# Weight slabs of the Fourier and convolution stage, split in the first feed forward and kept in DRAM as two parts

## The chip, the cores and the metric

The kernel runs on one core of one Trainium2 chip. The metric is device time in microseconds (us); 2587.58 us is the median of three runs of the kernel before (2584.76 to 2590.12).

## What is computed

Two blocks follow one another on a sequence of 512 positions and 1024 features. The first has two layers of attention. The second, where the change lies, has two layers: a mixer and a convolutional feed forward each. The mixer of its second layer is the Fourier and convolution stage. Cut to that layer, the reference is:

```python
h = _rmsnorm(x, norm_g[l, 0]) * (1.0 + scale) + shift
p = h @ cd_w_in                                # 1024 x 1536
y_c = _fourier_mix(p[..., :512])               # real part of a 2D FFT, 4 groups of 128
y_d = _conformer_conv(p[..., 512:], ...)       # val * sigmoid(gate), 31 taps, layer norm, silu
x = x + gate * (concat([y_c, y_d]) @ cd_w_out)
shift, scale, gate = _adaln(c, ada_w[l, 1], ada_b[l, 1])
h = _rmsnorm(x, norm_g[l, 1]) * (1.0 + scale) + shift
x = x + gate * _conv_ffn(h, ffn_w_up[l], ...)  # (silu(dwconv(u)) * v) @ w_down, 2816 wide
```

## The kernel before

All products run on TensorE in fp32r, and each factor is split into a high part (a cast on ScalarE) and a low part (a subtraction, mostly on VectorE). mm3 (L128) makes three products of these: high by high, high by low, low by high.

A weight slab is [128, 8, 128] in fp32, 512 KB. wslab (L70) loads it from SP's queue into wraw, casts it into whi (L75) and subtracts into wlo (L76). wraw, whi and wlo have three buffers each. gemm (L90) takes a slab, asks side() for one more step of waiting side work, and makes 24 matmuls of 512 columns into one of two pg buffers.

The order in which the kernel's text calls things is not the order on the engines. When the program is built, a planner sets one list for each engine and for SP's queue: among the instructions whose inputs and buffers it takes to be ready, the one earliest in the text goes first. On the chip each engine runs its list in order, and one that waits holds back what stands behind it.

The first feed forward (ffn, L1518, with l = 0) has two halves. Each makes eleven pairs of upward gemms (taps3 in L743 to L745, Silu in L1533, product in L1535, split into hidh and hidl) and then eight downward products. Beside it runs adaln (L710) as side work: 48 times a transfer of 512 KB into adaw (two buffers) and one reduction on VectorE (L719). They give the modulation that the norm at the feed forward's end needs. That norm (Norm, L239) prepares the first three slabs of the next stage in finish (L314), the third with its low part on GpSimd, between the high and low parts hh and hl of the normed input (L336, L344).

Then comes the Fourier and convolution stage (m3, L1834). conformer_in (L1411) makes eight gemms with slabs of cd_w_in; fourier (L1483) loads and splits the Fourier matrix into DH and DL in four pieces and makes four groups of one gemm, a product with CH and CL (split fuh, ful in L125) and a product with DH and DL; conformer_conv (L1428) makes the 31 taps on VectorE (cacc, L1451 and L1453), and 23 taps of the last channel on TensorE with diagonals (cdg, L1443 on GpSimd) that lie in the buffers of hh and hl; conformer_norm (L1458) follows. The projection with cd_w_out (out_proj_steps, L191) runs in two halves with half slabs (n = 4), the last three of the second half together. The loop over the two layers is at L1848.

Of the kernel before, what the change touches and what calls it, by code (L numbers as in the profile page):

```python
# [17 lines left out]
S = 512  # L18
# [6 lines left out]
class Ctx:  # L25
# [43 lines left out]

    def wslab(self, src, shape, raw=None, eng=None, out=None):  # L70
        nc = self.nc
        if raw is None:
            raw = self.wraw(src, shape)
        hi, lo = out or [self.w.tile(shape, F32R, name=t, tag=t) for t in ("whi", "wlo")]
        nc.scalar.activation(hi, raw, AF.Copy)  # L75
        (eng or nc.vector).tensor_tensor(lo, raw, hi.bitcast(F32), op=ALU.subtract)  # L76
        return hi, lo
# [113 lines left out]
    def out_proj_steps(self, pool, W, k0, mix, xcol, gate=None, done=None, norm=None, parts=None):  # L191
        nc, n = self.nc, len(mix)
        if parts is None:
            mh = pool.tile([128, n, S], F32R, name="mh")
            ml = pool.tile([128, n, S], F32R, name="ml")
            for k in range(n):
                self.split(mh[:, k, :], ml[:, k, :], mix[k])
        else:
            mh, ml = parts
        yield  # L200
        late = 0 if norm is None else norm.late if n == 8 else 3
        for o in range(KD - late):
            xc = xcol(o)
            ps = self.gemm(W[:, o, k0:k0 + n], mh, ml, n)
            self.add_x(xc, ps, gate, o)
            if done is not None:
                done(o, xc)
            if norm is not None:
                norm.tile(o)
            yield  # L210
        if norm is not None and not late:
            norm.finish()
        if late:
            last = range(KD - late, KD)
            ws = [self.wslab(W[:, o, k0:k0 + n], [128, n, 128]) for o in last]
            ps = [pp.tile([128, S], F32, name="pl", tag=tag) for pp, tag in ((self.pg, "pg"), (self.pg, "pg"), (self.px, "px"))[:late]]
            for hf, t in enumerate(HALVES):
                for j, o in enumerate(last):
                    self.products(ps[j], ws[j], (mh, ml), t, n)
                    self.add_x(xcol(o)[:, t], ps[j][:, t], gate, o)  # L220
                    norm.half(o, hf)
                if hf:
                    norm.begin()
                norm.stats(hf)
            norm.finish()
# [8 lines left out]
def at(x, k):  # L234

    return x[k] if isinstance(x, list) else x[:, k, :]


class Norm:  # L239
# [1171 lines left out]
def conformer_in(c, dp, hh, hl):  # L1411

    nc, I = c.nc, c.ins
    hds = []
    for j in range(4):
        ps = c.gemm(I["cd_w_in"][:, 8 + j], hh, hl)
        sg = c.t2("csg")
        nc.scalar.activation(sg, ps, AF.Sigmoid)
        ps = c.gemm(I["cd_w_in"][:, 4 + j], hh, hl)
        hd = dp.tile([128, S + 30], F32, name=f"chd{j}")  # L1420
        nc.gpsimd.memset(hd[:, 0:15], 0.0)
        nc.gpsimd.memset(hd[:, 527:542], 0.0)
        nc.vector.tensor_tensor(hd[:, 15:527], ps, sg, op=ALU.mult)
        hds.append(hd)
    return hds
# [57 lines left out]
def fourier(c, dp, hh, hl, mixf):  # L1483
# [1 line left out]
    DH = dp.tile([128, 8, S], F32R, name="DH")  # L1485
    DL = dp.tile([128, 8, S], F32R, name="DL")
    for z in range(4):
        raw = c.w.tile([128, 2, S], F32, name="wraw", tag="wraw")
        nc.sync.dma_start(raw, I["dft_s"][:, 2 * z:2 * z + 2])
        c.split(DH[:, 2 * z:2 * z + 2], DL[:, 2 * z:2 * z + 2], raw)  # L1490
    craw = c.load(dp, "dft_c", [128, 256])
    CH = dp.tile([128, 256], F32R, name="CH")
    CL = dp.tile([128, 256], F32R, name="CL")
    c.split(CH, CL, craw)
    for g in range(4):
        ps = c.gemm(I["cd_w_in"][:, g], hh, hl)
        uf = c.t2("fu")
        nc.scalar.activation(uf, ps, AF.Copy)
        uh = dp.tile([128, S], F32R, name="fuh", tag="fuh", bufs=2)
# [15 lines left out]

def ffn(c, fp, l, hh, hl, xT, norm):  # L1518
    nc, I = c.nc, c.ins
    gate = c.mod[l, 1][:, 2, :]  # L1520
    cw = fp.tile([128, NFF, 3], F32, name="fcw")
# [3 lines left out]
    for hf in range(2):  # L1525
        hid = []
        for jj in range(11):
            j = 11 * hf + jj
            ps = c.gemm(I["ffn_up"][l][:, 2 * j], hh, hl)
            p = padded(c, fp, ps)  # L1530
            u = c.t2("fu")
            taps3(c, u, p, cw[:, j, 0:1], cw[:, j, 1:2], cw[:, j, 2:3], cb[:, j:j + 1])
            nc.scalar.activation(u, u, AF.Silu)  # L1533
# [16 lines left out]

        for o in range(KD - late):
            c.side()
            w1 = c.wslab(W[:, o, k0:k0 + 8], [128, 8, 128])
            w2 = c.wslab(W[:, o, k0 + 8:k0 + 11], [128, 3, 128])
            ps = c.pg.tile([128, S], F32, name="pg", tag="pg")
# [36 lines left out]
def build(tc, I, out):  # L1592
    nc = tc.nc
    with ExitStack() as es:
# [238 lines left out]

        def m3(hh, hl, em, side, spec):  # L1834
            mixf = c.pool(em, "mixf", side).tile([128, KD, S], F32, name="mixf")
            W, gate = I["cd_w_out"], c.mod[1, 0][:, 2, :]
            mp = c.pool(em, "mp", side)
            with ExitStack() as e2:
                dp = c.pool(e2, "cd", side)
# [8 lines left out]
        for l, mx in enumerate((m2, m3)):  # L1848
            ex.close()
            prev = nm  # L1850
            with ExitStack() as em:
                mx(prev.hh, prev.hl, em, B, (*modulation(c, l, 1), [I["ffn_up"][l][:, k] for k in range(3)]))
            prev = nm
            if l == 0:
                nm = Norm(c, hp, xT, None, None, [I["cd_w_in"][:, k] for k in (8, 4, 9)])
            else:
                nm = Final(c, out, xT, gvec(I["final_g2"]), None, None)
            with ExitStack() as e2:
                fp = c.pool(e2, "ffn", B)
                if l == 0:  # L1860
                    sc = silu_c(fp)
                    place = lambda: fp.tile([128, 1024], F32, name="adaw", tag="adaw", bufs=2)
                    c.fill += [adaln(c, sc, 1, 0, place), adaln(c, sc, 1, 1, place)]
                for _ in ffn(c, fp, l, prev.hh, prev.hl, xT, nm):
                    if l == 0:
                        c.side(48)
                        nm.g, nm.shift = modulation(c, 1, 0)
# [178 lines left out]
```

## Time and profile before

| | |
|---|---|
| median of three runs | 2587.58 us (2584.76 to 2590.12) |
| profiled execution, its own time | 2596.75 us |
| its span | 2594.9 us |
| TensorE matmul busy | 2502.1 us (96%) |
| VectorE busy | 1681.6 us (65%) |
| ScalarE busy | 1063.4 us (41%) |
| GpSimd busy | 219.7 us (8%) |
| chain that ended last, by engine | TensorE 80%, VectorE 10%, ScalarE 3%, DMA 3%, GpSimd 2% |
| moved by DMA | 265.09 MB, 102 GB/s over the span |

The span runs from the first to the last instruction of one profiled execution, and all positions below are us from its start. Matmuls are pipelined: one of 512 columns lasts 0.40 us, while the next starts earlier, so counts and starts are read rather than the sum of durations. The feed forward of the first layer lies from 1630 to 2010, the Fourier and convolution stage from 2010 to 2200.

### The profile page before, as it was taken

What the parts mean: (1) busy time and instruction counts of PE and PEld (TensorE: products, weight loads), DVE (VectorE), ACT (ScalarE), POOL (GpSimd) and SP (SyncE); (2) the same over time, 40 slices, a digit from 0 to 9 for tenths busy, and PEclk for the clock granted to TensorE, in tenths of its full rate; (3) what the DMA queues carried; (4) which work ended last, traced back from release to release, by engine and by line L of the source; (5) the groups of instructions that cost most, each with busy time, mean ns of one, the idle gap of its engine ahead of it and who ended that gap; (6) DMA issues with size and microseconds to landing.
All of it is one profiled execution on the core that took longest, in us unless ns stands there. A gap on an engine that the chain in (4) does not pass through costs nothing.

```text
span 2594.9 us, 38956 instructions
## 1 busy us (share of the span) xinstructions
PE 2502.1 (96%) x15237; PEld 2006.4 (77%) x15237; DVE 1681.6 (65%) x3330; ACT 1063.4 (41%) x1903; POOL 219.7 (8%) x313
## 2 busy tenths in 40 slices
PE   8999999999999999999999988999999989999998
PEld 6769777787697777868677767878888767888887
DVE  5767666547677666586677676786444796543544
ACT  5653334536534335553433652532333424432331
POOL 0000111000001110201001130200000210100000
PEclk9999999999999999999999979999999989999999
DMA  4136111331372113311211322586334403223322
GB/s 149 44 132 236 57 57 57 106 107 37 111 259 62 58 54 106 106 57 57 89 40 56 125 96 82 191 265 207 101 87 122 148 1 101 76 87 102 96 82 80
DMA packets 91875, 265.09 MB, mean 102 GB/s; under 512 B 14372, under 2 KB 26924, under 8 KB 90796
## 3 DMA queue, kind: packets, MB, share of 16 engines
q1 hardware_dynamic: 91692, 262.61, 32.1%
q8 instruction: 120, 1.97, 0.3%
q14 instruction: 63, 0.52, 0.1%
HBM read 246.06 MB, written 16.52 MB: 101 GB/s over the span
## 4 chain that ended last, share of the span: by engine, by line
PE 80%; DVE 10%; ACT 3%; issue 3%; DMA 3%; POOL 2%; SPq 0%; ACTq 0%; DVEq 0%; POOLq 0%
PE pg L130 17%; PE pg L131 17%; PE pg L132 17%; DMA adaw<-in_ada_w_dram 2%; PE pgv L130 2%; PE pgv L132 2%; PE pgv L131 2%; DVE wlo L76 2%; PE po L683 1%; PE po L532 1%; PE tp L527 1%; PE sc L623 1%; PE po L688 1%; POOL hl L344 1%; PE phs L1364 1%
## 5 line engine op out<-in xcount | busy, mean ns | idle before, releaser
L75 ACT ACTIVATE whi<-wraw 128x1024 fp32r<-128x1024 f32 (+3 forms) x370 | 348.1, 942 | 751.6 <-PE pg L131 559.0
L130 PE MATMUL pg<-hh,whi 128*128 128x512 f32 x1560 | 630.9, 404 | 9.8 <-ACT whi L124 6.5
L131 PE MATMUL pg<-hl,whi 128*128 128x512 f32 x1560 | 629.6, 404 | 0.3 <-DVE hl L362 0.3
L132 PE MATMUL pg<-hh,wlo 128*128 128x512 f32 x1560 | 628.1, 403 | 0.0
L76 DVE TENSOR_TENSOR wlo<-wraw,whi 128x1024 fp32r<-128x1024 f32 (+4 forms) x366 | 420.9, 1151 | 272.4 <-ACT whi L75 265.3
L130 PEld LDWEIGHTS pg<-hh,whi 128*128 128x128 f32 x1560 | 295.2, 189 | 87.4 <-ACT whi L124 6.5
L131 PEld LDWEIGHTS pg<-hl,whi 128*128 128x128 f32 x1560 | 295.7, 190 | 77.6 <-issue 7.5
L132 PEld LDWEIGHTS pg<-hh,wlo 128*128 128x128 f32 x1560 | 295.6, 189 | 74.4 <-issue 4.5
L130 PE MATMUL pg<-hidh,whi 128*128 128x512 f32 (+1 forms) x396 | 148.1, 374 | 0.0
L132 PE MATMUL pg<-hidh,wlo 128*128 128x512 f32 (+1 forms) x396 | 146.2, 369 | 0.0
L131 PE MATMUL pg<-hidl,whi 128*128 128x512 f32 (+1 forms) x396 | 145.6, 368 | 0.0
L719 DVE CUSTOM_DVE_ANT_0 adaw<-adaw,sc 128x1024 f32<-128x1024 f32 x96 | 116.7, 1226 | 41.5 <-DMA adaw<-in_ada_w_dram 34.2
L591 POOL TENSOR_TENSOR shf<-shf,roped 128x512 f32<-128x512 f32 x48 | 61.8, 1287 | 532.8 <-ACT whi L75 250.1
L131 PE MATMUL pgv<-wlo,hh 128*128 128x512 f32 (+1 forms) x240 | 91.1, 380 | 0.0
L130 PE MATMUL pgv<-whi,hh 128*128 128x512 f32 (+1 forms) x240 | 90.6, 377 | 0.0
L132 PE MATMUL pgv<-whi,hl 128*128 128x512 f32 (+1 forms) x240 | 90.1, 375 | 0.0
L132 PEld LDWEIGHTS pg<-hidh,wlo 128*128 128x128 f32 x396 | 74.5, 188 | 15.2
L632 ACT ACTIVATE pp<-pp,nm 128x256 f32<-128x256 f32 x128 | 63.5, 497 | 54.6 <-DVE nm L629 54.6
L131 PEld LDWEIGHTS pg<-hidl,whi 128*128 128x128 f32 x396 | 74.4, 188 | 13.7
L130 PEld LDWEIGHTS pg<-hidh,whi 128*128 128x128 f32 x396 | 74.3, 188 | 13.5
L1533 ACT ACTIVATE fu<-fu 128x512 f32<-128x512 f32 x44 | 27.8, 632 | 116.1 <-DVE fu L745 116.1
L231 DVE SCALAR_TENSOR_TENSOR xT<-pg,mod,xT 128x512 f32<-128x512 f32 (+1 forms) x54 | 38.3, 711 | 50.0 <-PE pg L132 50.0
(524 smaller groups left out, 4530.2 us busy)
## 6 DMA issues: line engine op xcount, KB each, us to landing
adaw<-in_ada_w_dram SPq DMA_DIRECT2D x96, 512.0 KB, 4.7
wraw<-in_ffn_up_dram SPq DMA_DIRECT2D x88, 512.0 KB, 3.6
wraw<-in_w_dqk_dram SPq DMA_DIRECT2D x48, 512.0 KB, 3.6
wraw<-in_ffn_down_dram SPq DMA_DIRECT2D x32, 512.0 KB, 3.6
wraw<-in_w_dv_dram SPq DMA_DIRECT2D x24, 512.0 KB, 3.8
wraw<-in_w_gate_dram SPq DMA_DIRECT2D x16, 512.0 KB, 3.7
wraw<-in_w_out_dram SPq DMA_DIRECT2D x16, 512.0 KB, 3.7
wraw<-in_w_hg_dram SPq DMA_DIRECT2D x16, 512.0 KB, 3.7
```

Source lines behind the costliest of these rows:

```text
L75: nc.scalar.activation(hi, raw, AF.Copy)
L76: (eng or nc.vector).tensor_tensor(lo, raw, hi.bitcast(F32), op=ALU.subtract)
L130: mm(out, lhsT=ah, rhs=bh, start=first, stop=False)
L131: mm(out, lhsT=ah, rhs=bl, start=False, stop=False)
L132: mm(out, lhsT=al, rhs=bh, start=False, stop=last)
L231: self.nc.vector.scalar_tensor_tensor(x, in0=ps, scalar=gate[:, o:o + 1], in1=x, op0=ALU.mult, op1=ALU.add)
L344: nc.gpsimd.tensor_tensor(self.hl[:, k, t], u, h, op=ALU.subtract)
L527: nc.tensor.transpose(tp[:, kt, :], pe[:, kt * 128:(kt + 1) * 128], c.ident)
L591: nc.gpsimd.tensor_tensor(sh, sh, roped[:, 1, :], op=ALU.mult)
L632: nc.scalar.activation(pz, pz, AF.Exp, bias=nm[:, z, i:i + 1], scale=0.125, accum_out=st[:, 1, z, i:i + 1])
L719: nc.vector.tensor_tensor_reduce(w, in0=w, in1=sc, scale=1.0, scalar=0.0, op0=ALU.mult, op1=ALU.add, accum_out=mod[:, j:j + 1])
L1533: nc.scalar.activation(u, u, AF.Silu)
```

## The change

A class Parts holds two DRAM tiles for one slab. Its method make loads the slab into praw, splits it into phi and plo, and stores both; these three have two buffers each, in the feed forward's pool. While the first feed forward runs, the function ahead makes one slab after each of the 22 upward pairs' first gemm and before each of the 8 downward products of the first half, until the 24 are done: 12 slabs of cd_w_in, 4 pieces of the Fourier matrix, 8 slabs of cd_w_out. In the Fourier and convolution stage and in the norm before it, wslab then loads the two parts from DRAM straight into whi and wlo (or DH and DL), with no cast and no subtraction.

```diff
     def wslab(self, src, shape, raw=None, eng=None, out=None):
         nc = self.nc
+        if isinstance(src, Parts):
+            hl = out or [self.w.tile(shape, F32R, name=t, tag=t) for t in ("whi", "wlo")]
+            for t, z in zip(hl, src.parts):
+                nc.sync.dma_start(t.bitcast(F32), z)
+            return hl
         if raw is None:
             raw = self.wraw(src, shape)
...
+        slab = lambda o: W[o].cut(128, k0, k0 + n) if isinstance(W, list) else W[:, o, k0:k0 + n]
         for o in range(KD - late):
             xc = xcol(o)
-            ps = self.gemm(W[:, o, k0:k0 + n], mh, ml, n)
+            ps = self.gemm(slab(o), mh, ml, n)
...
+class Parts:
+    def __init__(self, c, src, name):
+        self.src = src.rearrange("p k n -> p (k n)")
+        self.parts = [c.dram.tile([128, 1024], F32, name=f"{name}{z}") for z in "hl"]
+
+    def make(self, c, pool):
+        raw = pool.tile([128, 1024], F32, name="praw", tag="praw", bufs=2)
+        c.nc.sync.dma_start(raw, self.src)
+        hl = [pool.tile([128, 1024], F32R, name=t, tag=t, bufs=2) for t in ("phi", "plo")]
+        c.split(*hl, raw)
+        for z, t in zip(self.parts, hl):
+            c.nc.sync.dma_start(z, t.bitcast(F32))
+
+    def cut(self, n, k0=0, k1=None):
+        v = Parts.__new__(Parts)
+        v.parts = [z.rearrange("p (k n) -> p k n", n=n)[:, k0:k1] for z in self.parts]
+        return v
...
-        ps = c.gemm(I["cd_w_in"][:, 8 + j], hh, hl)
+        ps = c.gemm(c.parts["in"][8 + j].cut(128), hh, hl)
...
     for z in range(4):
-        raw = c.w.tile([128, 2, S], F32, name="wraw", tag="wraw")
-        nc.sync.dma_start(raw, I["dft_s"][:, 2 * z:2 * z + 2])
-        c.split(DH[:, 2 * z:2 * z + 2], DL[:, 2 * z:2 * z + 2], raw)
+        c.wslab(c.parts["dft"][z].cut(S), None, out=[t[:, 2 * z:2 * z + 2] for t in (DH, DL)])
...
             ps = c.gemm(I["ffn_up"][l][:, 2 * j], hh, hl)
             p = padded(c, fp, ps)
+            if ahead is not None:
+                ahead()
             u = c.t2("fu")
...
             c.side()
+            if ahead is not None and not hf:
+                ahead()
             w1 = c.wslab(W[:, o, k0:k0 + 8], [128, 8, 128])
...
+                todo = [c.parts["in"][k] for k in (8, 4, 9, 5, 10, 6, 11, 7, 0, 1, 2, 3)] + c.parts["dft"] + c.parts["out"]
+                ahead = lambda: todo and todo.pop(0).make(c, fp)
+                nm = Norm(c, hp, xT, None, None, [c.parts["in"][k].cut(128) for k in (8, 4, 9)])
```

## Rows read from the trace of the kernel before

**Rows 1.** Stretches (us): length, busy us (instructions) of each engine, TensorE clock, DMA

```profile
1650.00:1800.00 150.00, 148.48 (x642) 118.43 (x641) 123.57 (x188) 45.76 (x63) 1.37 (x11) 1.00 0.78 251
1800.00:2000.00 200.00, 200.00 (x891) 162.04 (x890) 91.24 (x112) 60.70 (x81) 0.91 (x9) 1.00 0.36 106
2010.00:2031.00 21.00, 17.47 (x114) 16.07 (x113) 8.97 (x22) 15.81 (x35) 13.88 (x17) 0.84 0.52 187
2031.00:2109.00 78.00, 77.80 (x376) 63.36 (x374) 75.06 (x110) 27.02 (x43) 0.00 (x0) 1.00 0.25 78
...
735.00:755.00 20.00, 20.00 (x85) 20.00 (x85) 14.48 (x23) 5.76 (x7) 0.00 (x0) 1.00 0.99 365
...
1485.00:1495.00 10.00, 6.26 (x94) 4.99 (x92) 8.54 (x25) 9.45 (x13) 0.00 (x0) 0.97 1.02 403
```

**Rows 2.** Timeline of TensorE at the fourth slab: start, duration, what ran

```profile
2036.55 0.39 PE L130 MATMUL pg<-hh,whi 128*128 128x512 f32 x1
2036.78 0.40 PE L131 MATMUL pg<-hl,whi 128*128 128x512 f32 x1
```

**Rows 3.** Instructions by line and shape, VectorE, 2004 to 2192 us

```profile
L1453 DVE SCALAR_TENSOR_TENSOR cacc<-chd,l_dconv_w,cacc 128x512 f32<-128x512 f32 x97 | 67.6, 746 | 0.2
L76 DVE TENSOR_TENSOR wlo<-wraw,whi 128x1024 fp32r<-128x1024 f32 x11 | 13.3, 1221 | 2.0 <-ACT whi L75 2.0
L76 DVE TENSOR_TENSOR wlo<-wraw,whi 128x512 fp32r<-128x512 f32 x16 | 10.8, 683 | 0.0
...
L125 DVE TENSOR_TENSOR DL<-wraw,DH 128x1024 fp32r<-128x1024 f32 x4 | 4.9, 1224 | 0.3 <-ACT DH L124 0.2
```

**Rows 4.** Waits of TensorE, 1990 to 2230: us in total, times, longest

```profile
PE psf L132 <- DVE ful L125: 10.0, 2, 9.8
...
PE pg L130 <- ACT mh L124: 1.1, 1, 1.1
PE pe L116 <- POOL hl L344: 0.8, 3, 0.3
```

**Rows 5.** Waits of TensorE, 1600 to 1990

```profile
PE pg L130 <- DVE fu L1535: 1.4, 3, 0.6
```

**Rows 6.** Chain that ended last, 1655 to 1760: start, duration, what

```profile
1703.79 4.69 DMA adaw<-in_ada_w_dram
1708.51 1.22 DVE adaw L719
...
1743.35 0.61 DVE fu L1535
```

**Rows 7.** Timeline of GpSimd, 2018 to 2121

```profile
2021.10 2.37 POOL L76 TENSOR_TENSOR wlo<-wraw,whi 128x1024 fp32r<-128x1024 f32 x1
2023.43 5.78 POOL L344 TENSOR_TENSOR hl<-u,hh 128x256 fp32r<-128x256 f32 x8
...
2109.22 6.27 POOL L1443 TENSOR_TENSOR cdg<-c_ident,cwh 128x2944 fp32r<-128x2944 f32 x1 [80.00 <-PE pg L132]
2115.45 5.58 POOL L1443 TENSOR_TENSOR cdg<-c_ident,cwl 128x2944 fp32r<-128x2944 f32 x1
```

**Rows 8.** Timeline of ScalarE at the projection's second half

```profile
2172.43 0.63 ACT L75 ACTIVATE whi<-wraw 128x512 fp32r<-128x512 f32 x1 [2.17 <-PE pg L131]
```

**Rows 9.** Timeline of VectorE at the diagonals

```profile
2110.59 5.47 DVE L125 TENSOR_TENSOR cdg<-chd,cdg 128x542 fp32r<-128x542 f32 x1
2115.99 5.59 DVE L125 TENSOR_TENSOR ful<-fu,fuh 128x512 fp32r<-128x512 f32 x1
```

**Rows 10.** Transfers of adaw, 1600 to 1800

```profile
DMA to landing us min/median/max: 3.5/4.5/5.9
```

**Rows 11.** DMA issues: times, KB each, median us to landing

```profile
wraw<-in_cd_w_out_dram SPq DMA_DIRECT2D x16, 256.0 KB, 2.7
```

**Rows 12.** Instructions by line and shape, VectorE, 1650 to 1800 us

```profile
L719 DVE CUSTOM_DVE_ANT_0 adaw<-adaw,sc 128x1024 f32<-128x1024 f32 x47 | 57.5, 1224 | 20.4 <-DMA adaw<-in_ada_w_dram 20.1
```

**Rows 13.** Transfers of adaw, 0 to 1500

```profile
DMA to landing us min/median/max: 3.6/6.1/7.6
```

More of the change, by code (lines that the diff above doesn't have):

```diff
@@ L214, in out_proj_steps @@
             last = range(KD - late, KD)
-            ws = [self.wslab(W[:, o, k0:k0 + n], [128, n, 128]) for o in last]
+            ws = [self.wslab(slab(o), [128, n, 128]) for o in last]
             ps = [pp.tile([128, S], F32, name="pl", tag=tag) for pp, tag in ((self.pg, "pg"), (self.pg, "pg"), (self.px, "px"))[:late]]
@@ L1415, in conformer_in @@
     for j in range(4):
-        ps = c.gemm(I["cd_w_in"][:, 8 + j], hh, hl)
+        ps = c.gemm(c.parts["in"][8 + j].cut(128), hh, hl)
         sg = c.t2("csg")
         nc.scalar.activation(sg, ps, AF.Sigmoid)
-        ps = c.gemm(I["cd_w_in"][:, 4 + j], hh, hl)
+        ps = c.gemm(c.parts["in"][4 + j].cut(128), hh, hl)
         hd = dp.tile([128, S + 30], F32, name=f"chd{j}")
@@ L1495, in fourier @@
     for g in range(4):
-        ps = c.gemm(I["cd_w_in"][:, g], hh, hl)
+        ps = c.gemm(c.parts["in"][g].cut(128), hh, hl)
         uf = c.t2("fu")
@@ L1514, in fourier, with ffn @@
         nc.scalar.activation(mixf[:, g, :], ps, AF.Copy)
-def ffn(c, fp, l, hh, hl, xT, norm):
+def ffn(c, fp, l, hh, hl, xT, norm, ahead=None):
     nc, I = c.nc, c.ins
@@ L1835, in m3 @@
             mixf = c.pool(em, "mixf", side).tile([128, KD, S], F32, name="mixf")
-            W, gate = I["cd_w_out"], c.mod[1, 0][:, 2, :]
+            W, gate = c.parts["out"], c.mod[1, 0][:, 2, :]
             mp = c.pool(em, "mp", side)
@@ L1853, in build @@
             prev = nm
+            ahead = None
             if l == 0:
-                nm = Norm(c, hp, xT, None, None, [I["cd_w_in"][:, k] for k in (8, 4, 9)])
+                c.parts = {n: [Parts(c, I[w][:, a * k:a * k + a] if n == "dft" else I[w][:, k], n + str(k)) for k in range(m)]
+                           for n, w, a, m in (("in", "cd_w_in", 1, 12), ("dft", "dft_s", 2, 4), ("out", "cd_w_out", 1, 8))}
+                todo = [c.parts["in"][k] for k in (8, 4, 9, 5, 10, 6, 11, 7, 0, 1, 2, 3)] + c.parts["dft"] + c.parts["out"]
+                ahead = lambda: todo and todo.pop(0).make(c, fp)
+                nm = Norm(c, hp, xT, None, None, [c.parts["in"][k].cut(128) for k in (8, 4, 9)])
             else:
@@ L1863, in build @@
                     c.fill += [adaln(c, sc, 1, 0, place), adaln(c, sc, 1, 1, place)]
-                for _ in ffn(c, fp, l, prev.hh, prev.hl, xT, nm):
+                for _ in ffn(c, fp, l, prev.hh, prev.hl, xT, nm, ahead):
                     if l == 0:
```

## Prediction

> **What bounds the kernel now.** I read the table of stretches first. In the first feed forward (1650 to 2000 us) TensorE is busy 148.5 of 150 and 200.0 of 200 us; in the part of the Fourier and convolution stage whose slabs the change touches (2031 to 2109) it is busy 77.8 of 78 [rows 1]. A matmul of 512 columns starts 0.23 us after the one before it [rows 2], so a slab of 24 matmuls takes 5.6 us. VectorE is nearly full in the same place, 75.1 of 78 us [rows 1]: the convolution's taps alone are 97 instructions of 0.746 us (67.6 us), and between them lie the low parts of the slabs [rows 3]. This looks like a VectorE bound, but TensorE loses nothing there. So I read next what TensorE waits for. From 1990 to 2230 the one large wait is 10.0 us, for ful in L125; the waits for mh (1.1 us) and for the low parts hl (0.8 us) are small [rows 4]. In the feed forward it waits 1.4 us in three times for fu of L1535 [rows 5]. The chain of waits goes there through a transfer of adaw (4.69 us), its reduction on VectorE (1.22 us) and the next transfer, and leaves VectorE at 1743.35 [rows 6]: for some 75 us that loop is as long as TensorE's own work.
>
> **What is taken away.** On VectorE 11 low parts of 1.221 us, 16 of half slabs of 0.683 and 4 of the Fourier matrix of 1.224: 13.4 + 10.9 + 4.9 = 29.2 us; on GpSimd one of 2.37 us [rows 3, 7]; on ScalarE as many casts. Where TensorE waits for none of that, the gain is nothing. I find four places.
>
> (a) Head, 2010 to 2031. GpSimd makes the low part of the third slab at 2021.10, and the last eight hl follow it [rows 7]. Without it they come 2.3 us earlier. TensorE waits for hl only 0.8 us in all [rows 4], and is at 0.84 of its clock there, busy 17.5 of 21 us [rows 1]. Bounds 0 and -2.3; I take -1.0, the wait and a little of what follows it.
>
> (b) First Fourier group. Its ful stands on VectorE behind a low part of 1.22 us. Bounds 0 and -1.2, I take -0.5, since TensorE has other products to put between.
>
> (c) Second half of the projection. ScalarE stands 2.17 us at 2172.43 for a slab buffer that TensorE still reads, and the four mh are queued behind that cast [rows 8]. Loaded slabs need no cast, so mh comes as soon as the Silu is done. TensorE's wait for mh goes (-1.1) [rows 4], with a little behind it: -1.6, bounds 0 and -2.3. Next late is the first half's last product, which is TensorE's own work.
>
> (d) The wait of 10.0 us. When the last product on hh and hl is done, GpSimd builds the two diagonals in the same buffers, 6.27 and 5.58 us from 2109.22 [rows 7]. VectorE's two subtractions that start meanwhile take 5.47 and 5.59 us and end with them, against 0.68 of the like size [rows 3, 9]. Nothing of that is split off by the change, and ful cannot exist before the product that also frees GpSimd. I take 0; the bounds stand with the rival.
>
> **What is added in this stage.** Each slab now comes as two transfers into whi and wlo themselves, which can only start when TensorE has left the buffer. A transfer of 512 KB lands in 4.5 us [rows 10], the second one about 1.4 us later (0.524 MB at 365 GB/s [rows 1]); the slab three further on is needed 11.2 us later, so 5 us are left. Half slabs land in 2.7 us [rows 11] plus some 0.7 and have 5.6; only the last, which is wanted with two others after 24 products of half width (2.8 us), may cost 0.6 at most; I take 0.3. The danger is the start. DH and DL (4.2 MB) no longer wait for a raw buffer and come free with the feed forward's last product at about 2010, and they would then stand in SP's queue right behind slabs two and three (2.1 MB), with xd and xT (2.6 MB), ahead of slab four (1.05 MB): 10 MB, which take 25 to 27 us at 403 or 365 GB/s [rows 1], till about 2035 to 2037. Slab four is wanted at 2036.55 [rows 2], its buffer is free at about 2029, when the last hl is made [rows 7]. Bounds 0 and +5; I take +0.8, since the buffer comes free in time and the rates bracket the need.
>
> **What is added in the first feed forward.** 24 loads, 24 casts, 24 subtractions and 48 stores of 0.524 MB: 37.7 MB, and 24 x 1.22 = 29.3 us on VectorE [rows 3]. Eleven fall to its first half's upward slabs, eight to its downward ones, five to the second half (the planner may run them earlier, two at a time). From 1650 to 1800 VectorE is busy 123.6 of 150 us, 57.5 of it the 47 reductions of adaw, and DMA moves 251 GB/s; from 1800 to 2000 it is 91 of 200 us at 106 GB/s [rows 1, 12]. There is room for all of it in the sum (26 idle us in the first stretch, 109 in the second), but not at the old pace: two upward slabs (11.2 us) now have two wraw and four adaw, 3.15 MB; with one slab made ahead that is 4.72 MB, or 421 GB/s, where the two densest stretches reach 365 and 403 [rows 1]. So adaw must go slower, and nothing wants it before the second half. The DMAs are all on SP's queue, in order: behind a store that waits for plo stand the next wraw and adaw. The wraw is asked for some three slabs early, which covers one such wait. Who is not covered is VectorE: behind an adaw that is late stand the taps, fu and hidl, and TensorE waits for fu. Bounds: -1.4, if the slower pace takes away the three waits [rows 5]; and +12, if the eleven subtractions of the upward part (13.4 us) all land on the chain less the 1.4 already waited. A nearer row is the stretch from 735 to 755, where DMA is full (0.99), adaw runs beside slab loads, and TensorE is still busy 20.0 of 20 us [rows 1]. So I take +1.5.
>
> Sum: -1.0 - 0.5 - 1.6 + 0 + 0.3 + 0.8 + 1.5 = **-0.5 us**. The profiled execution took 2596.75 us (span 2594.9), 9.2 above the median of the runs, 2587.58; the terms are differences, so I put them on the median: **2587 us**, no change that can be told. I call 0.2% (5.2 us) what a measurement here can tell.
>
> The Trainium skill's page HBM Reference, section Specifications (TRN2), says that a core that streams alone measures well above its share of 358, about 425 GB/s. By it the 421 would just pass and the slow rival below would lose its price; the rows show 365 over 20 us and 403 over 10 [rows 1], so I keep that rival.
>
> **The rivals.** *Slower: the loop of adaw.* Its place is the upward part, 1660 to 1760. A loop of transfer and reduction takes 4.69 + 1.22 = 5.9 us and serves one of two buffers, so two adaw pass in 5.9 us where a slab takes 5.6; the excess of 0.3 us per slab used up some 2 us of slack before TensorE first waited. In the earlier use of adaw, beside a full DMA, the median landing is 6.1 against 4.5 us here [rows 10, 13]. If the planned order still holds two reductions per slab, the loop is 1.6 us longer, the excess 1.9 us, and the slack gone in two slabs; over the ten or twelve slabs left that is 19 to 23 less the 2: about +19, so 2606. It decides once adaw lands later than about 5 us without being spread. For it: the chain goes through this loop now. Against: the full stretch at 735, and that the order is planned anew with the added transfers in it. *Slower: the head.* The 10 MB in front of slab four cost the upper bound and the late half slabs the same again: +6, 2593. *Faster: the 10 us.* With 13 full and Fourier low parts (15.9 us) gone before 2109, VectorE has the taps behind it. If ful is then put ahead of the cdg subtraction, it ends with GpSimd's first diagonal rather than the second, -5.6 [rows 7, 9], or TensorE gets some projection products to fill the wait, 9 of 0.23 us or -2. With (a) to (c) and nothing lost in the feed forward: -3.1 - 5.6 = -8.7, so 2579. Against: the cast for cdg needs one step less than that for ful, so cdg is ready first. *No effect at all:* the slabs are loaded either way; that is inside the likeliest case.
>
> **How the numbers follow.** Chances: no change to tell 0.47 (2582.4 to 2592.8), the loop 0.20 (2594 to 2612), the head 0.10, faster 0.23 (2576 to 2582). So faster 0.23, same 0.47, slower 0.30. The range of 8 in 10 runs from 2578, which leaves out the last fifth of the fast case, to 2606, which leaves out the upper half of the loop's.
>
> **What would show it.** Right: VectorE 15 us less busy between 2031 and 2109 with TensorE full in both; no wait for mh at the second half of the projection; ful and cdg still above 5 us each; adaw spread over more than the 145 us it has now, and waits for fu of L1535 within a few us. Wrong: those waits above 8 us with adaw landing at 6 us or more (the loop); a wait of the fourth slab's first product, or of any, for a transfer into whi or wlo (the head); ful down to one diagonal's time, or ahead of GpSimd (the fast case). The prediction fails also if the new order, which is planned for the whole program, brings a wait at a place that the change does not touch.

## The result, and the profile after

The changed kernel takes 2613.93 us (median of four, 2611.97 to 2621.34) where the kernel before, run beside it, takes 2588.85: a ratio of 1.0100, 95% interval 1.0085 to 1.0114. It is 25 us slower; the forecast was 2587, and its range ended at 2606. The profiled execution took 2613.28 us (span 2611.5). The helpers' lines stand five further down: whi and wlo are L80 and L81, mm3's products L135 to L137; the taps are L1479 and L1481.

Up to the first transfer that the change adds, at 1615 us, both kernels hold the same instructions in the same order on every engine, but for seven neighbouring pairs of small matmuls that overlap. So the two profiled executions can be compared by TensorE's matmuls of the same rank, 15237 in each. At 1615 the kernel after is 9.8 us ahead, which the change can't have caused: the execution profiled of the kernel before is a long one of its kind, 2596.75 us. At the feed forward's end the two are level (0.1 apart), at the end of the projection the kernel after is 18.5 us behind, and from the next feed forward on 17.1. So 9.8 us are lost in the feed forward, all of it among the first half's downward products, and 18.5 in the stage, of which 1.4 come back right behind it. TensorE's waits name the places: total us, times, longest. First the answer to [rows 5], 1600 to 1990:

```profile
PE pg L135 <- ACT whi L80: 4.3, 4, 1.5
PE pg L137 <- DVE wlo L81: 3.8, 5, 1.5
```

and the answer to [rows 4], 1990 to 2230:

```profile
PE psf L137 <- DVE ful L130: 9.2, 1, 9.2
PE psb L166 <- DVE rsy L153: 6.5, 3, 2.7
PE pg L136 <- DVE ml L130: 6.4, 1, 6.4
PE pg L135 <- ACT mh L129: 5.1, 1, 5.1
PE pst L160 <- DVE sqa L179: 2.0, 1, 2.0
PE pe L117 <- DMA whi<-in4h: 1.3, 1, 1.3
```

Two places. In the feed forward TensorE waits 8.1 us for the two parts of its own slabs, which it did not before; the waits for fu [rows 5] are gone. At the projection it waits 6.4 us for ml, 5.1 for mh and 2.0 for sqa; ml stands on VectorE among the last taps, sqa and mh come from the layer norm behind them. The wait for ful is nearly what it was [rows 4].

The stretches of [rows 1] again, VectorE's busy time in the third group of figures:

```profile
1650.00:1800.00 150.00, 144.66 (x607) 114.38 (x606) 109.61 (x147) 58.07 (x73) 0.92 (x9) 0.99 0.92 324
...
2031.00:2109.00 78.00, 77.52 (x364) 62.14 (x363) 37.83 (x64) 15.06 (x32) 1.00 (x1) 1.00 0.51 186
```

From 2031 to 2109 VectorE is busy 37.8 us against 75.1 [rows 1], which is 37 us less. The low parts that the change takes from there account for 16 of these (9 slabs of 1.22 us and the Fourier matrix). Besides, 34 of the 78 taps that ran there, 25 us, have left the stretch, and some 4 us of other work have come in. In all there are as many taps as before, 97 of 744 ns (the answer to [rows 3]). VectorE's timeline (start, duration, what ran, idle time before) shows where they went, with the taps' first input chd, the first tap and the last:

```profile
2029.92 0.69 DVE L1451 TENSOR_TENSOR chd<-pe,csg 128x512 f32<-128x512 f32 x1 [8.91 <-PE pe L121]
...
2074.31 0.99 DVE L1479 TENSOR_SCALAR cacc<-chd,l_dconv_w,l_dconv_b 128x512 f32<-128x512 f32 x2
...
2167.35 0.74 DVE L1481 SCALAR_TENSOR_TENSOR cacc<-chd,l_dconv_w,cacc 128x512 f32<-128x512 f32 x1
```

The first tap starts at 2074.3 though its input chd is written at 2029.9. The taps also read the convolution's weights and bias, two small loads. SP's queue in the kernel after:

```profile
2063.26 0.32 SPq L75 DMA_DIRECT2D whi<-in2h  x1
2063.67 0.38 SPq L75 DMA_DIRECT2D wlo<-in2l  x1
2064.11 0.42 SPq L58 DMA_DIRECT2D l_dconv_w<-in_dconv_w_dram  x1
2068.86 0.32 SPq L75 DMA_DIRECT2D whi<-in3h  x1
2069.27 0.38 SPq L75 DMA_DIRECT2D wlo<-in3l  x1
2069.70 0.42 SPq L58 DMA_DIRECT2D l_dconv_b<-in_dconv_b_dram  x1
```

the same loads in the kernel before:

```profile
2008.82 0.33 SPq L58 DMA_DIRECT2D l_dconv_w<-in_dconv_w_dram  x1
...
2011.15 1.01 SPq L58 DMA_DIRECT2D l_dconv_b<-in_dconv_b_dram  x1
```

and its first tap on VectorE:

```profile
2032.11 0.55 DVE L1451 TENSOR_SCALAR cacc<-chd,l_dconv_w,l_dconv_b 128x512 f32<-128x512 f32 x1
```

They are issued 55 and 59 us later. What holds SP's queue is shown by its own waits in the kernel after, 2004 to 2110:

```profile
SPq L75 <- PE pg L137: 64.6, 12, 12.3
SPq L75 <- PE pe L118: 11.2, 2, 9.8
SPq L75 <- PE pg L136: 9.9, 1, 9.9
SPq L75 <- PE pe L121: 6.3, 3, 3.2
```

92 of 106 us SP stands before a load into whi or wlo (L75) until TensorE has left the buffer. Before, slabs went to wraw, which a cast and a subtraction empty early; now each load waits for the end of a product, and everything behind it in the queue waits too. The Trainium skill, page "DMA: Bandwidth & Descriptors", section "Anatomy of one DMA — SWDGE (gpsimd) path", says that DMA engines don't wait on semaphores and that any such wait happens on the issuing sequencer before dispatch. These rows of SP's queue agree with it, and a load of 2 KB is among those that stand behind.

### The profile page after: what moved, and what is told of

The parts are those of the page before. It is cut to its first block, busy times and chain, and to the rows that moved or that the text cites. A ratio compares the mean times of both kernels' runs of the same rounds, so it can differ in the third digit from the quotient of the medians.

```text
span 2611.5 us, 39065 instructions
## 1 busy us (share of the span) xinstructions
PE 2498.3 (96%) x15237; PEld 1999.7 (77%) x15237; DVE 1681.5 (64%) x3323; ACT 1063.7 (41%) x1895; POOL 215.9 (8%) x312
## 4 chain that ended last, share of the span: by engine, by line
PE 79%; DVE 10%; ACT 4%; issue 3%; DMA 2%; POOL 2%; SPq 0%; DVEq 0%; ACTq 0%; POOLq 0%
PE pg L135 18%; PE pg L136 17%; PE pg L137 17%; PE pgv L135 2%; PE pgv L136 2%; PE pgv L137 2%; PE po L711 1%; PE po L560 1%; DVE wlo L81 1%; PE tp L555 1%; PE sc L651 1%; PE po L716 1%; DMA praw<-in_dft_s_dram 1%; DVE cacc L1481 1%; POOL hl L372 1%
## 5 line engine op out<-in xcount | busy, mean ns | idle before, releaser
L135 PE MATMUL pg<-hh,whi 128*128 128x512 f32 x1560 | 631.1, 405 | 9.7 <-ACT whi L129 6.7
L137 PE MATMUL pg<-hh,wlo 128*128 128x512 f32 x1560 | 628.6, 403 | 0.6 <-DVE wlo L81 0.4
L80 ACT ACTIVATE whi<-wraw 128x1024 fp32r<-128x1024 f32 (+3 forms) x342 | 324.7, 952 | 618.5 <-PE pg L136 460.3
L81 DVE TENSOR_TENSOR wlo<-wraw,whi 128x1024 fp32r<-128x1024 f32 (+4 forms) x339 | 396.9, 1172 | 227.5 <-ACT whi L80 221.6
L135 PEld LDWEIGHTS pg<-hh,whi 128*128 128x128 f32 x1560 | 295.8, 190 | 85.4 <-ACT whi L129 6.7
L137 PEld LDWEIGHTS pg<-hh,wlo 128*128 128x128 f32 x1560 | 296.0, 190 | 76.0 <-issue 4.5
L135 PE MATMUL pg<-hidh,whi 128*128 128x512 f32 (+1 forms) x396 | 148.5, 375 | 3.1 <-ACT whi L80 3.1
L137 PE MATMUL pg<-hidh,wlo 128*128 128x512 f32 (+1 forms) x396 | 147.4, 372 | 3.8 <-DVE wlo L81 3.8
L137 PEld LDWEIGHTS pg<-hidh,wlo 128*128 128x128 f32 x396 | 74.8, 189 | 20.7 <-DVE wlo L81 5.9
L135 PE MATMUL pgv<-whi,hh 128*128 128x512 f32 (+1 forms) x240 | 89.6, 373 | 0.0
L137 PE MATMUL pgv<-whi,hl 128*128 128x512 f32 (+1 forms) x240 | 88.9, 370 | 0.0
L135 PEld LDWEIGHTS pg<-hidh,whi 128*128 128x128 f32 x396 | 74.9, 189 | 17.9 <-ACT whi L80 4.4
L136 PE MATMUL pg<-ml,whi 128*128 128x512 f32 x164 | 66.5, 406 | 6.4 <-DVE ml L130 6.4
```

Of the source, the lines that this page charges most:

```text
L135: mm(out, lhsT=ah, rhs=bh, start=first, stop=False)
L136: mm(out, lhsT=ah, rhs=bl, start=False, stop=False)
L137: mm(out, lhsT=al, rhs=bh, start=False, stop=last)
```

## Experiments

Each ratio is against the kernel before, run beside it on the same chip (medians 2589.2 to 2591.0 us); 0.0010 is 2.6 us. Theory A had two parts: late taps cost about 18 us, and the splitting in the downward products about 8.

**Small loads first.**

```diff
 dp = c.pool(e2, "cd", side)
+pre = [c.load(dp, n, s) for n, s in (("dconv_w", [128, 4, 31]), ("dconv_b", [128, 4]),
+       ("dconv_ln_g", [128, 4]), ("dconv_ln_b", [128, 4]))]
 cv = conformer_in(c, dp, hh, hl)
...
-    cw = c.load(dp, "dconv_w", [128, 4, 31])
-    cb = c.load(dp, "dconv_b", [128, 4])
```

> The changed kernel with one edit: the four small loads of the convolution (its weights, its bias and the two vectors of its layer norm) are asked for at the head of the Fourier and convolution stage, ahead of its slabs. Theory A (late taps): in the changed kernel the two loads that the taps need stand on SP's queue behind slab loads that wait for TensorE to leave whi and wlo; they are issued at 2064.1 and 2069.7 us instead of 2008.8 and 2011.2, so VectorE's first tap starts at 2074.3 instead of 2032.1 and the last ends at about 2168 instead of 2142. With the loads early the first tap stands at about 2031 and the 17 to 19 us that the stage lost come back: 2614 - 18 = 2596 us, +7 against the kernel before. What is left is the first feed forward. Rival B (the stage is slow because slabs of twice the bytes are loaded straight into buffers that TensorE reads, or because of the diagonals): the taps may start early, but the stage stays 17 us longer, 2613.

Measured: 2591.8 us, ratio 1.0016 (1.0003 to 1.0029), so 0.0084 or 21.7 us come back, 5 more or less by the two intervals. The first tap is where it was in the kernel before:

```profile
2032.07 0.55 DVE L1477 TENSOR_SCALAR cacc<-chd,l_dconv_w,l_dconv_b 128x512 f32<-128x512 f32 x1
```

The waits for ml and sqa are gone, and 0.8 us is left of that for mh; TensorE's waits 1990 to 2230 begin with

```profile
PE psf L137 <- DVE ful L130: 8.8, 1, 8.8
PE psb L166 <- DVE rsy L153: 5.9, 2, 3.3
PE pe L117 <- ACT hh L364: 0.8, 1, 0.8
PE pg L135 <- ACT mh L129: 0.8, 1, 0.8
```

Rival B falls: slabs of twice the bytes, loaded straight into the buffers, cost TensorE no wait in the stage that shows here.

**One late load in the kernel before.** The opposite test, with nothing of the change in it.

```diff
+        if not g:
+            nc.scalar.activation(dp.tile([128, 4], F32, name="late", tag="late", bufs=1), uf[:, 0:4], AF.Copy)
...
-    cb = c.load(dp, "dconv_b", [128, 4])
+    cb = c.load(dp, "dconv_b", [128, 4], tile=dp.tile([128, 4], F32, name="late", tag="late", bufs=1))
```

> The kernel before with one wait added and nothing of the change: the buffer of the convolution's bias (2 KB) is first written with four columns of the first Fourier group, so its load, and with it every tap, can't start before about 2070 us. TensorE waits for none of that directly. Theory A (late taps are a sufficient cause): the taps that VectorE runs from 2032 to 2073 today, some 40 of 0.67 to 0.75 us (27 to 30 us), move behind; VectorE has still 29 us of low parts there, which may now stand before the taps. The low parts of the projection and the layer norm come late, and the time rises by 17 to 30 us, 2606 to 2619. Rival B (VectorE has slack, the stage of the changed kernel is slow for its transfers): 2589, no change.

Measured: 2615.43 us, ratio 1.0100 (1.0078 to 1.0121): one load of 2 KB made late costs as much as the whole change, 20 to 31 us by the interval; by matmuls of the same rank the trace has 19 to 21. The first tap is at 2068.36. The layer norm's two vectors and the weights were loaded early here, so the bias alone is enough. The waits for ml and mh appear at the projection, with a third for low parts:

```profile
PE pg L131 <- DVE ml L125: 5.9, 1, 5.9
PE pg L130 <- ACT mh L124: 5.1, 1, 5.1
PE pg L132 <- DVE wlo L76: 3.8, 1, 3.8
```

**Where the splitting stands.** Three runs: the changed kernel without splitting in the downward products, the same with the small loads first, and the kernel before with the parts made and not used.

```diff
             if ahead is not None:
                 ahead()
+                if hf and jj < 2:
+                    ahead()
...
-            if ahead is not None and not hf:
-                ahead()
```

> The changed kernel with the splitting ahead left out of the first half's downward products; it goes with the upward slabs of both halves alone (one per pair, two at the first two pairs of the second half). Theory A: in the first half's downward products, 1750 to 1808 us, SP's queue runs a loop of praw's landing (some 5.8 us), cast (1.06), subtraction (1.23) and the store that waits for it, 8.6 us, and the slab loads of the next product stand in the same queue behind that store, while a product of TensorE takes 7.7; so TensorE waits for whi and wlo, some 8 us in all. Without it: 2614 - 8 = 2606. Rival B: the feed forward's loss is the loop of adaw in the upward part, or VectorE's added 29 us wherever they stand: no gain here, 2614, or a new loss in the second half.

> Both edits: small loads of the convolution first, and no splitting in the downward products. If both theories A hold and the two losses add up, 2614 - 18 - 8 = 2588, the time of the kernel before within 3 us; less than that only if the stage now gains from VectorE's 29 us less. If only the late taps count, 2596; if only the downward products, 2606.

> The changed kernel with the parts made in the first feed forward as there, but not used: the stage loads its raw slabs and splits them as the kernel before does. So it is the kernel before plus the work of making. Theory A (the two losses are apart: some 8 us in the downward products of the feed forward, 17 to 18 in the stage): +8, 2597. Rival B (all of the loss is the stage's): 2589. Rival C (the making costs more than 8, and the stage gave part of it back): 2600 or more.

Measured: 2604.23 us, 1.0062 (1.0046 to 1.0078); 2582.38, 0.9975 (0.9963 to 0.9987); 2600.41, 1.0045 (1.0029 to 1.0062). Taking the splitting out of the downward products gives 0.0038 without the small loads and 0.0041 with them, 10 and 11 us; the small loads give 0.0084 with that splitting and 0.0087 without it, about 22 us both times. The making alone costs 11.7. The losses add up, and without both the change is faster than the kernel before by 0.25%, which I had named only as the lesser possibility.

**The stage alone.**

```diff
+                del todo[1:]
                 ahead = lambda: todo and todo.pop(0).make(c, fp)
```

(and all Parts share the first one's two DRAM tiles, with the small loads first. So 23 of the 24 splittings are left out, and the stage multiplies with one slab's parts throughout.)

> The changed kernel with the small loads of the convolution first, and with only one slab split ahead in the feed forward; all 24 slabs of the stage load that one pair of parts, so 23 of the 24 splittings are left out and the stage computes with the wrong weights. It tells what the stage gains by itself, with its transfers and waits as in the change. Theory A: the making costs 9 to 11 us and all of it in the downward products, so this takes 2592 - 9 to 11 = 2581 to 2583, the same as the run that held small loads first and no splitting in the downward products (2582). Rival B: making costs something in the upward products too; then this is 2 or more below that run, 2580 or less. Rival C: the stage gains nothing: 2589.

Measured: 2581.72 us, 0.9968 (0.9955 to 0.9981). The stage with its new transfers is worth some 8 us (4.9 to 11.7), against the run with the splitting in the upward products 0.9975: between theory A and rival B, with intervals that overlap. So splitting in the upward products costs 2 us by these medians, and by the intervals anything from nothing to 6.

**Order or bytes in the downward products.** I had two readings of the 10 us there: SP's queue, where a store waits for its cast and the next slab's load stands behind it, or the bytes. Four runs. First the stores on another queue:

```diff
-            c.nc.sync.dma_start(z, t.bitcast(F32))
+            c.nc.gpsimd.dma_start(z, t.bitcast(F32))
```

> The changed kernel with the small loads first, the splitting kept in the downward products, and only the stores of the two parts issued from GpSimd's queue in place of SP's. It tells whether the feed forward's loss is the order of SP's queue (loads of the next slab and of praw behind a store that waits for plo) or the bytes: a downward product of 7.7 us has 0.72 MB of slab, 0.52 of praw, 1.05 of parts to store and 0.52 of adaw, 2.8 MB or 365 GB/s, where the stretch 1740 to 1810 moved 324 with DMA busy 0.95. Theory A (order): the loop is cut, the waits for whi and wlo go, 2592 - 9 = 2583. Rival B (bytes): the slabs land as late as before, 2592. Above 2592, GpSimd's queue would have a cost of its own.

Measured: 2618.44 us, 1.0104 (1.0085 to 1.0123), 23 us over the same kernel with the stores on SP's queue. It did not answer the question. Freed from SP's order, the planner packed the splitting closer: the 17th of the 24 slabs is stored from 1755.6 on, among the upward products, where on SP's queue that store stands at 1795.5. The stretch 1650 to 1800:

```profile
1650.00:1800.00 150.00, 132.56 (x528) 103.31 (x526) 113.36 (x155) 58.01 (x73) 22.83 (x52) 0.94 1.01 396
```

TensorE's longest wait in it, and VectorE's:

```profile
PE pg L135 <- DVE fu L1559: 12.7, 5, 4.7
```

```profile
DVE adaw L747 <- DMA adaw<-in_ada_w_dram: 11.7, 8, 2.5
```

DMA is full at 396 GB/s, VectorE waits for adaw, and TensorE for the fu behind it: this is the slower rival of the prediction, with its place and about its price, since by matmuls of the same rank the upward part takes 19 us longer than in the kernel before. In the changed kernel, where the stores stand in SP's queue, the splitting is spread further and this did not happen. Whether stores from GpSimd's queue have a cost of their own besides is not shown. The Trainium skill's page "DMA: Bandwidth & Descriptors", section "Issuing engines are not separate DMA queues", says that DMAs from all engines run on the same 16 DMA engines; the full DMA here agrees.

Then praw asked for one place earlier, so that the stores find their cast done:

```diff
+    def get(self, c, pool):
+        self.raw = pool.tile([128, 1024], F32, name="praw", tag="praw", bufs=2)
+        c.nc.sync.dma_start(self.raw, self.src)
...
-                ahead = lambda: todo and todo.pop(0).make(c, fp)
+                def ahead(started=[]):
+                    if todo:
+                        started.append(todo.pop(0))
+                        started[-1].get(c, fp)
+                    if len(started) > 1 or started and not todo:
+                        started.pop(0).make(c, fp)
```

> The changed kernel with the small loads first, the splitting kept in the downward products, the same bytes on the same queue; but praw of each slab is asked for one place earlier than it is split. So in SP's queue of a downward product the order is praw of the next slab, the two stores of this one, the loads of the next product, adaw, and the stores no longer wait for a praw that was asked for just before them. It tells apart the two readings of the feed forward's loss, which the run with the stores on GpSimd's queue left open because its planner drew all of the splitting into the upward products. Theory A (order): the loop of landing, cast, subtraction and store is no longer in series with the slab loads; the waits for whi and wlo (some 8 us) fall below 2 us, 2592 - 8 = 2584. Rival B (bytes): 2.8 MB per product of 7.7 us stay 365 GB/s; the slabs land as late, 2592.

Measured: 2592.94 us, 1.0014 (1.0002 to 1.0027), no change against 1.0016. SP's wait for casts of praw fell from 39.0 to 6.1 us between 1740 and 1815, but SP then stood 22.4 us for a wraw buffer. So two more, the first with buffers of its own for the small raw slab, the second with short stores as well:

```diff
+                r3 = fp.tile([128, 3, 128], F32, name="wraw3", tag="wraw3", bufs=2)
+                nc.sync.dma_start(r3, W[:, o, k0 + 8:k0 + 11])
-            w2 = c.wslab(W[:, o, k0 + 8:k0 + 11], [128, 3, 128])
+            w2 = c.wslab(W[:, o, k0 + 8:k0 + 11], [128, 3, 128], raw=r3)
...
-            c.nc.sync.dma_start(z, t.bitcast(F32))
+            c.nc.sync.dma_start(z[:, 0:n], t[:, 0:n].bitcast(F32))
```

> Small loads first and praw asked for one place earlier, as in the run before; and in the downward products the raw slab of three blocks gets two buffers of its own, so that the three wraw buffers hold slabs of eight blocks alone and can be asked for further ahead. In the run before, SP stood 22.4 us between 1740 and 1815 for a wraw buffer in place of the 39 us for a cast of praw, and the loss stayed. Theory A' (order, in a wider sense: any wait of SP in that stretch makes the slab loads late): with both waits gone the waits for whi and wlo fall below 2 us, 2592 - 8 = 2584. Rival B (bytes: a product of 7.7 us has 2.8 MB, 365 GB/s, above what the stretch moved in any run, 310 to 331): the slabs land at 7 us as before, 2592.

> The same as that run, with the two stores of each slab split in the downward products cut to an eighth (128 of 1024 columns); the stage reads another slab's parts for these, so it computes with the wrong weights. Everything else of the order and the waits stays; a product has 1.9 MB in place of 2.8. Rival B (bytes): the slabs land in about 4.5 us as in the kernel before, the waits for whi and wlo go, 2592 - 8 = 2584. Theory A' (order), if the run with deeper buffers still has the loss: no change against that run.

Measured: 2593.13 us, 1.0008 (0.9996 to 1.0020), and 2585.88, 0.9978 (0.9966 to 0.9990). Buffers alone leave most of the loss; without most of the stores' bytes (an eighth is stored, and the stage reads another slab's parts instead) it is gone, and the time is that of no splitting there (0.9975). The stretch 1740 to 1815 with the buffers alone, and the slabs' transfers in it (times, KB, median us to landing):

```profile
1740.00:1815.00 75.00, 69.00 (x293) 54.28 (x292) 47.85 (x65) 26.45 (x32) 0.21 (x2) 1.00 0.97 343
```

```profile
wraw<-in_ffn_down_dram SPq DMA_DIRECT2D x8, 512.0 KB, 6.0
```

The same two views with short stores:

```profile
1740.00:1815.00 75.00, 73.69 (x315) 58.76 (x314) 53.45 (x72) 26.68 (x33) 0.21 (x2) 1.00 0.87 292
```

```profile
wraw<-in_ffn_down_dram SPq DMA_DIRECT2D x8, 512.0 KB, 4.0
```

With the full bytes DMA is 0.97 busy and the slabs land in 6 us; with fewer they land in 4.0, as in the kernel before (4.1 in that stretch), and TensorE is busy 73.7 of 75 us. So the stores' bytes decide, and not how long SP stands: its waits in this stretch come to 45 us with the buffers alone and to 46 with short stores. A busy share of 0.91 is no loss by itself either, as the run with both edits has it there, at 315 GB/s, with TensorE busy 75.0 of 75. One part of the order is not separated from the bytes: SP's wait for plo, which precedes a store, is 27.0 us with full stores and 14.4 with short ones, and a short store also gives its buffer back sooner.

**The ten microseconds of ful.** On top of the run with both edits:

```diff
-        uf = c.t2("fu")
-        nc.scalar.activation(uf, ps, AF.Copy)
+        uf = ps
+        if g < 3:
+            uf = c.t2("fu")
+            nc.scalar.activation(uf, ps, AF.Copy)
```

> Small loads first and no splitting in the downward products, as in the run that held both; and in the last Fourier group the high part and ful are taken from the product in PSUM itself, without the copy fu. It tells what the wait of 8.8 us for ful is. Theory A (VectorE's subtraction of two tensors in SBUF stands still while GpSimd builds the diagonals, and behind the subtraction for cdg): with an operand in PSUM ful takes some 0.7 us and its cast is ready one step earlier, ahead of cdg's: the wait falls from 8.8 to 1 or 2 us, 2582 - 7 = 2575. Rival B (the subtraction is held whatever its operands, or cdg's still goes first): 2582.

Measured: 2585.93 us, 0.9984 (0.9973 to 0.9995), not faster than 0.9975. VectorE's timeline there:

```profile
2104.31 0.69 DVE L130 TENSOR_TENSOR ful<-pg,fuh 128x512 fp32r<-128x512 f32 x1
2104.91 4.91 DVE L130 TENSOR_TENSOR cdg<-chd,cdg 128x542 fp32r<-128x542 f32 x1
2109.74 5.59 DVE L1479 SCALAR_TENSOR_TENSOR cacc<-chd,l_dconv_w,cacc 128x512 f32<-128x512 f32 x1
```

GpSimd's:

```profile
2103.81 5.43 POOL L1469 TENSOR_TENSOR cdg<-c_ident,cwh 128x2944 fp32r<-128x2944 f32 x1 [80.58 <-PE pg L137]
2109.20 5.58 POOL L1469 TENSOR_TENSOR cdg<-c_ident,cwl 128x2944 fp32r<-128x2944 f32 x1
```

and two of TensorE's waits, 1990 to 2230:

```profile
PE psf L135 <- DVE fal L1533: 5.1, 1, 5.1
PE pcv L135 <- POOL cdg L1469: 2.2, 1, 2.2
```

The first half of theory A holds: ful from PSUM takes 0.69 us while GpSimd builds its first diagonal. The second half fails: cdg and one tap, each with two operands in SBUF, then stand for 4.9 and 5.6 us, and the next thing behind them, fal, is late in ful's place. The Trainium skill's page "SBUF — State Buffer", section "SBUF: two separate sides", has the rule for these rows: an operation of VectorE with two inputs in SBUF and one of GpSimd that reads SBUF lock each other out for the whole instruction. The wait belongs to GpSimd's diagonals and not to ful.

**What the freed VectorE is worth.** In the run with both edits VectorE waits 4.7 and 13.6 us behind its last taps. So more of the fourth channel group's 31 taps go to it from TensorE and GpSimd: 31 (no diagonals at all), 20, 25, and 20 in the kernel before.

```diff
-CT = 8
+CT = 20
```

> Small loads first and no splitting in the downward products; and the fourth channel group's convolution wholly on VectorE: 23 more taps there, and no diagonals on GpSimd, no cdg and no 69 matmuls on TensorE. It tells whether the 29 us that the change takes from VectorE can be put to use. In the run that held both, VectorE waits 4.7 and 13.6 us after the last taps while TensorE multiplies the diagonals. Theory A: TensorE loses 69 x 0.233 = 16 us of work and most of the 8.8 us wait, VectorE gains 23 x 0.75 = 17 us of taps and loses some 10 us of held subtractions; the layer norm then is next late and takes back part: about -18, 2564. Rival B: VectorE becomes the bound as in the changed kernel, the low parts and the layer norm come as late as there: 2582 or more.

> The same with the split of the fourth channel group in between: 20 of its 31 taps on VectorE and 11 on TensorE, instead of 8 and 23. TensorE loses 36 x 0.233 = 8.4 us of work, GpSimd's diagonals fall from 5.4 and 5.6 us to 2.6 and 2.7 by their size, and so the wait for ful from 8.8 to about 4: 2582 - 13 = 2569, VectorE's 12 taps (9 us) being covered by its idle time. If VectorE has no room, 2582 or more.

> Small loads first, no splitting in the downward products, and 25 taps of the fourth channel group on VectorE. Between 20 (2574, no wait for the second half's mh above 0.8 us) and 31 (2575.5, with waits for rsy 6.7, mh 5.1 and sqa 3.2 us). TensorE loses another 15 x 0.233 = 3.5 us and GpSimd's diagonals another 2.5; VectorE gains 5 x 0.75 = 3.7. If VectorE has that room still, 2574 - 4 to 5 = 2570; if it is full at 20 already, 2574.

> The kernel before, with 20 of the 31 taps of the fourth channel group on VectorE in place of 8, nothing else. It is the control for the run in which 20 taps on VectorE together with the mended change took 2574. Theory A (the time comes from VectorE's 29 us that the change sets free): here VectorE has no room, its last tap is at 2142 and would come at about 2146, the layer norm behind it as late as now, so what TensorE saves (8.4 us of matmuls and 5 of the wait for ful) comes back as a wait for the second half of the projection: 2589 within 4. Rival B (the split of the taps was simply badly chosen): 2589 - 13 = 2576.

Measured: 2575.51 us, 0.9939 (0.9920 to 0.9957); 2573.92, 0.9939 (0.9922 to 0.9956); 2572.41, 0.9929 (0.9914 to 0.9944); and in the kernel before 2596.21, 1.0017 (1.0003 to 1.0030). The three on top of both edits gain another 9 to 12 us over 0.9975; with 31 and 20 taps that is less than the 18 and 13 expected, with 25 it is what was expected. There is no difference among them that the intervals carry. The same edit in the kernel before gains nothing, as theory A had it. TensorE's first waits 1990 to 2230, with 31, with 25, and with 20 in the kernel before:

```profile
PE psb L166 <- DVE rsy L153: 6.7, 3, 2.7
PE pg L135 <- ACT mh L129: 5.1, 1, 5.1
PE pst L160 <- DVE sqa L179: 3.2, 1, 3.2
```

```profile
PE psb L166 <- DVE rsy L153: 6.1, 2, 3.5
PE pg L135 <- ACT mh L129: 2.3, 1, 2.3
PE psf L137 <- DVE ful L130: 2.2, 1, 2.2
```

```profile
PE pg L131 <- DVE ml L125: 8.7, 2, 8.4
PE psb L161 <- DVE rsy L148: 4.8, 2, 2.6
PE psf L132 <- DVE ful L125: 4.7, 1, 4.7
```

With 31 mh and sqa, which VectorE's work precedes, are late again. The wait for ful shrinks with the diagonals, from 8.8 us to 4.3 with 20 taps and 2.2 with 25, and is gone with 31, where there are none. In the kernel before, what TensorE saves comes back at once as a wait for ml.

## Why the prediction was wrong

The change cost 25.9 us (in ratios times 2589 us). Undone one after the other, the late small loads are +21.7 of it, the splitting in the downward products +10.6, and all the rest -6.5. That the three make up the whole is arithmetic; that the parts are real shows in the other order, which gives 22.5 and 9.8, and in the trace, with 18.5 lost in the stage, net of what it gains, and 9.8 in the feed forward. The prediction's sum was -0.5.

**The step that failed** is the one on slabs that are loaded into whi and wlo themselves. It saw that such a load "can only start when TensorE has left the buffer" and then asked only whether the slab comes in time, which it does. It did not ask what else stands on SP's queue behind that wait. For the feed forward the prediction did write that all DMAs are on SP's queue in order; in the stage it counted only what stands ahead of slab four. The small loads were not in its rows at all. With them the price could have been bounded: no tap runs without l_dconv_b, whose load would come when the last Fourier slab finds its buffer, near 2070; VectorE ran 36 taps ahead of 2075, 26.5 us in the kernel before, and these move behind. Nor did the step on what is taken away say how its cover could go: VectorE was "nearly full" and TensorE lost nothing, because the taps ran under the gemms. Its sign to watch, VectorE 15 us less busy from 2031 to 2109, came out at 37 with TensorE full, and that was the mark of the loss, not of the gain. The prediction's last caveat, a wait at a place that the change does not touch, is nearest to what came.

**The feed forward** was right in kind and wrong in place and size: +1.5 with bounds -1.4 to +12, measured +10.6 by the runs and 9.8 in the trace. The term that was mis-sized is the downward products, to which it gave no price of their own. It worked out the rate for the upward products alone (421 GB/s). For a downward product of 7.7 us the same sum gives 0.72 MB of slab, 0.52 of praw, 1.05 of stores and 0.52 of adaw, 365 GB/s, where the stretch 1740 to 1815 carried 326 to 343 in the runs with that load. The row it leaned on, 735 to 755, shows a full DMA for 20 us; it could not speak for 60. In the upward products the planner spread adaw, from 1637 to 1911 as forecast, and the three waits for fu went: the rival of adaw's loop did not happen, and the run with the stores on GpSimd's queue shows that it was one planner's choice away. The prediction cited the Trainium skill's page HBM Reference, section Specifications (TRN2), for about 425 GB/s of a core that streams alone. No run here tests that figure, since loads and stores ran together; with both, 396 GB/s with DMA full was the most that 150 us of any run carried, with a loss.

**The smaller terms.** In the trace, between the run with parts made and not used and the run with small loads first, which split alike, the stage gains some 5 us by matmuls of the same rank: 1.4 in the head (forecast -1.0 for the third slab's low part), 0.4 in the Fourier groups (-0.5), about 3 around the diagonals, where the wait for ful falls from 10.3 to 8.8 us and the convolution's products start earlier (0), and little at the second half of the projection, where the wait for mh falls from 1.1 to 0.8 (-1.6). So their sum of -3.1 was too small by 2, and its parts were misplaced. The start of the DMAs (+0.8) shows as one wait of 1.3 us for whi of the second slab, not the fourth. The faster rival, ful ahead of cdg, was tried in another form and brings nothing, since the standstill moves to the next instruction.

## What to carry to other kernels

When a load gets a new wait, list what stands behind it on its queue, down to loads of a few KB, and for each who reads it and how much work hangs on that; issue small constants ahead of anything that can block. A busy engine that the critical one doesn't wait for may be full of work that has to be done early: if that engine falls idle after a change, look for the work that left. Time freed on an engine off the path is worth little until work is moved to it: here 0.25% without that, 0.7% with 25 of 31 taps in place of 8.

## What the hardware did that I had not expected

Stores to DRAM delay the loads beside them: with full stores, DMA at 0.97 and 343 GB/s, slabs landed in 6.0 us; with the stores cut to an eighth they landed in 4.0, as in the kernel before (4.1). Around TensorE's waits for sqa, rsy and mh its granted clock is 0.59 on average over the 16 us from 2176, mostly the lower of its two levels (1.2 and 2.4 GHz), with 7 us of work in them, and it is 0.89 in the 18 us of full work that follow. In the kernel before it is 1.00 from 2130 to 2200.

```profile
2176.00:2192.00 16.00, 6.99 (x25) 5.46 (x24) 9.19 (x22) 6.74 (x11) 0.00 (x0) 0.59 0.13 45
2192.00:2210.00 18.00, 18.00 (x86) 14.99 (x84) 7.29 (x12) 3.58 (x6) 0.00 (x0) 0.89 0.45 147
```

So the late taps cost more than the waits show: TensorE's waits from 1990 to 2230 are 12 us longer in total (32.4 against 20.1, all of them added), the stage 18.5 us, by matmuls of the same rank. Some 4 of the 6 us between are the clock's: from 2100 to 2215, 22 matmuls of 512 columns start 0.43 us after the one before, against 4 of them in the kernel before, where 0.23 is the usual step. The rest is not traced.
